# Softmax quotients on GpSimd, two heads in one tile, and another placing of DSA's top-k rounds

## The chip, the cores and the metric

One core of a Trainium2 chip runs the whole kernel. The metric is device time in microseconds, the median of several runs; lower is better. The engines named here are TensorE (PE; its weight loads are shown as PEld), VectorE (DVE), ScalarE (ACT), GpSimd (POOL) and SyncE (SP), which issues the loads.

## The reference, cut to what matters

Two layers; each is a half-step SwiGLU FFN, a mixer of three attention groups, and a second FFN. Sequence length is 256, width 1024, sixteen heads of 64.

```
x = x + 0.5 * swiglu(rmsnorm(x, ffn1_norm), ...)
h = rmsnorm(x, mix_norm);  p = h @ w_in
  A (8 heads): window of 128 keys, learned sink in the softmax sum
  B (4 heads): MoBA; with 256 keys this is plain causal attention
  C (4 heads): DSA; score = sum_h relu(q_idx_h . k_idx) * w_idx_h
               idx = top_k(score, 64 keys); softmax over those keys only
  softmax: e = exp(s - m);  o = (e / sum(e)) @ v
x = x + concat(A, B, C) @ w_out
x = x + 0.5 * swiglu(rmsnorm(x, ffn2_norm), ...)
```

The choice of 64 keys is made in eight rounds on a score tile `acc`: a round finds the eight largest of each row and overwrites them with a marker. After the eighth round the marked places are the chosen keys.

## The kernel before, in words

All arithmetic is in float32. A weight chunk of 128x1024 is split into a high part (`whi`, a cast on ACT) and a low part (`wlo`, a subtraction on DVE that reads `raw` and `whi`), three chunks ahead of its products on PE. The FFNs are long rows of such products (`pgu`, `pdn`).

The mixer (`mix`) is written as one order of work. First come the products for the values (`pv`), five projections (`pp`), and the four index heads (`pi`, `r`, `acc`). Then a loop goes over eight pairs of heads, i = 0 to 7. In one pass of it, `score(i)` issues the score products `psc` on PE, the sum with the bias and the row extreme on DVE (`sb`, `nm`), and the exponentials on ACT (`e`, with the row sums `den`). `values(i-2)` multiplies the transposed weights with the values (`po`) and copies them out (`ohl`). `work(n)` lets PE go on with a number of steps of the remaining projections, later of the output product (`pp`, `pwo`); twelve such steps lie in one pass. `flip(i-1)` transposes the divided exponentials of the previous pair on PE (`pt`, six transposes) and copies them on ACT (`et`). `take(n)` runs rounds of the key choice on DVE. `normalise(i)` adds the sink's term (`es`, `ee`, `dn`), takes the reciprocal `rd`, and divides the exponentials: four DVE instructions per pair, in line 580, two heads by two query blocks. The wider block holds 256 keys and the other 128, so one head's `e` has 384 columns.

Pairs 6 and 7 are group C. Their biases `bs` are the bias plus the mask `sel` made from the finished `acc` (POOL, line 536; `chosen` in line 490). In the pass with the last round, `sel` and the biases of pair 6 are issued. The latent of group C (`latent`) runs beside the loop in three steps: the square `sq` on ACT and `cg` on DVE, then its row sum `pss` and the products `pk` on PE, then `kc` and its values.

Each engine works through its own instructions strictly in program order. That order is made from the code's order when the kernel is built: the scheduler may pull an instruction forward on its engine, but once built it is fixed, and an instruction that waits holds up those behind it. PE's instructions are chained in the order of the code.

Of the kernel before, what the change touches and what calls it, by code (L numbers as in the profile page):

```python
# [10 lines left out]
F32 = mybir.dt.float32  # L11
F32R = mybir.dt.float32r
AF = mybir.ActivationFunctionType
OP = mybir.AluOpType

P = 128
# [12 lines left out]
NKEEP = min(256, T // 4)  # L29
# [15 lines left out]
PRE = 6  # L45
FILL = [12] * 8 + [3, 3, 6]

TAKES = [2, 2, 1, 1, 1, 1, 0, 0]


_QA, _KA, _VA, _QB, _KB, _VB, _QC, _CKV, _QI, _KI, _WI = (
# [26 lines left out]
def tile_trunk(ctx, tc, xT, gains, kvg, sinks, table, onehot, wgu, wdn, winv, wins, wkv, wout, out):  # L78
    nc = tc.nc
# [4 lines left out]
    tmp = ctx.enter_context(tc.tile_pool(name="tmp", bufs=3))  # L84
# [3 lines left out]
    def bank(name, tag="mm"):  # L88
        return psum.tile([P, 512], F32, tag=tag, name=name)
# [100 lines left out]
    ident = const.tile([P, P], F32, name="ident")  # L190
# [15 lines left out]
    def in_order(ins):  # L206
        last_pe[0] = behind(ins, last_pe[0])

    def matmul(*a, **kw):
        in_order(nc.tensor.matmul(*a, **kw))  # L210

    def transpose(*a):
        in_order(nc.tensor.transpose(*a))  # L213
# [155 lines left out]
    bias = const.tile([P, NH, 2 * P], F32, name="bias")  # L369
# [34 lines left out]
    def mix(l, norm, nxt):  # L404

        pv = [bank("pv"), bank("pv")]
        for k in range(DK):
            if k % 2 == 0:
                whi, wlo = next_w()
            c = slice(k % 2 * VCOLS, (k % 2 + 1) * VCOLS)  # L410
# [48 lines left out]
        blocks = ((1, slice(0, T)), (0, slice(T, T + P)))  # L459
# [19 lines left out]
        def take(rounds):  # L479

            for _ in range(rounds):
                for b, cs in blocks:
                    m8 = tmp.tile([P, 8], F32, tag="m8", name="m8", bufs=4)
                    nc.vector.max(out=m8, in_=acc[:, cs])  # L484
                    nc.vector.match_replace(out=acc[:, cs], in_to_replace=m8, in_values=acc[:, cs], imm_value=TAKEN)  # L485

        def chosen():

            sel = tmp.tile([P, 3 * P], F32, tag="sel", name="sel", bufs=1)
            nc.vector.tensor_scalar(sel, acc, TAKEN, NEG, op0=OP.is_gt, op1=OP.mult)  # L490
            return sel
# [25 lines left out]
        nms, dens, ets, sels = {}, {}, {}, {}  # L517
        es_, state = {}, {}

        def qkv(j):  # L520
            h = HEADS[j]
            if h < NA:
                return halves(pr[f"qa{h % 4}"], h // 4), halves(pr["ka"], h // 4), h // 4
            i = h % 4
            if h < NA + NB:
                return halves(pr[f"qb{i // 2}"], i), halves(pr[f"kb{i // 2}"], i), 2 + i
            return halves(pr[f"qc{i // 2}"], i), halves(pr["kc"], i), 6
# [13 lines left out]
        def score(i):  # L541

            nms[i] = tmp.tile([P, 2, 2], F32, tag="nm", name="nm", bufs=3)
            dens[i] = tmp.tile([P, 2, 2], F32, tag="den", name="den", bufs=3)
            ps = [bank("psc", "at") for _ in range(2)]
            both = [qkv(2 * i + m) for m in range(2)]
            for p, (q, k, _) in zip(ps, both):
                matmul(p[:, 0:T], q[:, P:T], k[:, 0:T], start=True, stop=True)
            for p, (q, k, _) in zip(ps, both):
                matmul(p[:, T:T + P], q[:, 0:P], k[:, 0:P], start=True, stop=True)  # L550
            es_[i] = []
            for m, p in enumerate(ps):
                j = 2 * i + m
                sb = tmp.tile([P, 3 * P], F32, tag="A", name="sb")
                for (b, cs), bt in zip(blocks, sels.pop(j)):
                    nc.vector.tensor_tensor_reduce(  # L556
                        out=sb[:, cs], in0=p[:, cs], in1=bt, scale=-1.0,
                        scalar=BIG if j >= NA else nsink[:, l * NA + j:l * NA + j + 1],
                        op0=OP.add, op1=OP.min, accum_out=nms[i][:, b, m:m + 1])
                e = tmp.tile([P, 3 * P], F32, tag="E", name="e", bufs=4)  # L560
                for b, cs in blocks:
                    nc.scalar.activation(e[:, cs], sb[:, cs], AF.Exp, scale=-1.0, bias=nms[i][:, b, m:m + 1],  # L562
                                         accum_out=dens[i][:, b, m:m + 1])
                es_[i].append(e)

        def normalise(i):
            den = dens[i]
            if 2 * i < NA:
                es = tmp.tile([P, 2, 2], F32, tag="es", name="es", bufs=2)
                c = l * NA + 2 * i  # L570
                nc.vector.tensor_add(es, nms[i], sink[:, None, c:c + 2].to_broadcast([P, 2, 2]))
                ee = tmp.tile([P, 2, 2], F32, tag="ee", name="ee", bufs=2)
                nc.scalar.activation(ee, es, AF.Exp)
                den = tmp.tile([P, 2, 2], F32, tag="dn", name="dn", bufs=2)
                nc.vector.tensor_add(den, dens[i], ee)
            rd = tmp.tile([P, 2, 2], F32, tag="rd", name="rd", bufs=2)
            nc.vector.reciprocal(rd, den)
            for m, e in enumerate(es_[i]):
                for b, cs in blocks:
                    nc.vector.tensor_scalar(e[:, cs], e[:, cs], rd[:, b, m:m + 1], None, op0=OP.mult)  # L580

        def flip(i):

            ets[i] = []
            pts = [bank("pt", "at") for _ in range(2)]
            for pt, e in zip(pts, es_.pop(i)):
                for n, c in enumerate((2, 0, 1)):
                    transpose(pt[:, n * P:(n + 1) * P], e[:, c * P:(c + 1) * P], ident)
            for pt in pts:
                et = tmp.tile([P, 3 * P], F32, tag="ET", name="et", bufs=4)  # L590
                nc.scalar.copy(et, pt[:, :3 * P])
                ets[i].append(et)
# [52 lines left out]
        def work(n):  # L645
            for _ in range(n):
                next(fill, None)

        lat = None
        work(PRE)  # L650
        for i in range(NPAIR):
            for j in (2 * i, 2 * i + 1):
                if j not in sels:
                    biases(j)
            score(i)
            if i > 1:
                values(i - 2)
            n = FILL[i]
            work(n // 2)
            if i:  # L660
                flip(i - 1)
            take(TAKES[i])
            if i == len(TAKES) - TAKES[::-1].index(next(t for t in TAKES[::-1] if t)) - 1:
                state["sel"] = chosen()
                biases(NA + NB)
                biases(NA + NB + 1)
            normalise(i)
            if lat is None and "ckv" in pr:
                lat = latent()
            if lat:  # L670
                next(lat, None)
            work(n // 4)
            if lat:
                next(lat, None)
            work(n - n // 2 - n // 4)
# [8 lines left out]
        for k in range(DK):  # L684
            for i in range(LASTK):
                n = k * LASTK + i
# [127 lines left out]
```

## Time and profile before

| quantity | value |
|---|---|
| median of 3 runs | 981.63 us (979.8 to 982.25) |
| the profiled execution | 978.45 us |
| its span | 976.7 us |
| PE busy | 955.7 us, 98% of the span |
| DVE busy | 703.9 us, 72% |
| ACT busy | 536.9 us, 55% |
| POOL busy | 166.0 us, 17% |

The profile is of one execution. Busy time is summed over a whole span, so a share says little on a stage: the mixer of layer 0 lies at 200 to 297 us, that of layer 1 at 676 to 774 us, and the rest is FFN. In the lists below a line gives an instruction's start, its length, engine, line of the kernel, what it writes and reads with the tile's shape, and in brackets how long the engine had been idle before it and what ended that.

### The profile page before, as it was taken

What the parts mean: (1) busy time and instruction counts of PE and PEld (TensorE: products, weight loads), DVE (VectorE), ACT (ScalarE), POOL (GpSimd) and SP (SyncE); (2) the same over time, 40 slices, a digit from 0 to 9 for tenths busy, and PEclk for the clock granted to TensorE, in tenths of its full rate; (3) what the DMA queues carried; (4) which work ended last, traced back from release to release, by engine and by line L of the source; (5) the groups of instructions that cost most, each with busy time, mean ns of one, the idle gap of its engine ahead of it and who ended that gap; (6) DMA issues with size and microseconds to landing.
All of it is one profiled execution on the core that took longest, in us unless ns stands there. A gap on an engine that the chain in (4) does not pass through costs nothing.

```text
span 976.7 us, 15686 instructions
## 1 busy us (share of the span) xinstructions
PE 955.7 (98%) x5920; PEld 845.4 (87%) x5920; DVE 703.9 (72%) x1307; ACT 536.9 (55%) x988; POOL 166.0 (17%) x169
## 2 busy tenths in 40 slices
PE   8999999999999999999999999999999999999996
PEld 6888888898898888888888888889988988888885
DVE  5877776669956877776668777665797578787552
ACT  6655555445656656554456555544465576565442
POOL 3211110100103211211122212111002042122111
PEclk9999999999999999999999999999999999999998
DMA  9697555553434555555545555555433445555511
GB/s 339 232 310 262 205 173 181 183 186 115 142 107 138 209 195 194 176 210 174 199 151 211 176 206 181 177 179 185 150 130 99 161 143 202 197 191 178 208 46 43
DMA packets 47575, 174.41 MB, mean 179 GB/s; under 512 B 3291, under 2 KB 5867, under 8 KB 47372
## 3 DMA queue, kind: packets, MB, share of 16 engines
q1 hardware_dynamic: 47212, 172.90, 51.5%
q8 instruction: 46, 0.75, 0.3%
q10 hardware_dynamic: 288, 0.52, 0.1%
q14 instruction: 29, 0.24, 0.1%
HBM read 172.34 MB, written 4.22 MB: 181 GB/s over the span
## 4 chain that ended last, share of the span: by engine, by line
PE 86%; DVE 6%; ACT 3%; issue 2%; POOL 2%; DMA 1%; SPq 0%; POOLq 0%; DVEq 0%; ACTq 0%
PE pgu L210 46%; PE pdn L210 25%; PE pp L210 6%; PE pwo L210 4%; PE pv L210 2%; DVE wlo L153 2%; ACT whi L152 2%; PE po L210 1%; PE psc L210 1%; PE pt L213 1%; POOL ss L240 1%; POOL rcol L255 1%; DVE acc L485 1%; DMA raw<-wgu 1%; DVE m L484 1%
## 5 line engine op out<-in xcount | busy, mean ns | idle before, releaser
L210 PE MATMUL pgu<-xx,whi 128*128 128x512 f32 x1408 | 494.8, 396 | 2.1 <-DVE xx L230 1.6
L153 DVE TENSOR_TENSOR wlo<-raw,whi 128x1024 fp32r<-128x1024 f32 (+2 forms) x322 | 388.5, 1208 | 147.4 <-ACT whi L152 140.0
L152 ACT CAST whi<-raw 128x1024 fp32r<-128x1024 f32 (+2 forms) x322 | 332.7, 1035 | 254.0 <-PE pdn L210 109.2
L210 PE MATMUL pgu<-xx,wlo 128*128 128x256 f32 x1408 | 395.2, 281 | 0.2 <-DVE wlo L153 0.2
L210 PEld LDWEIGHTS pgu<-xx,whi 128*128 128x128 f32 x1408 | 264.1, 188 | 64.5 <-ACT whi L152 3.4
L210 PEld LDWEIGHTS pgu<-xx,wlo 128*128 128x128 f32 x1408 | 266.3, 189 | 1.1 <-DVE wlo L153 1.0
L210 PE MATMUL pdn<-h,whi 128*128 128x512 f32 x704 | 248.1, 397 | 0.0
L210 PE MATMUL pdn<-h,wlo 128*128 128x256 f32 x704 | 197.5, 281 | 0.0
L210 PEld LDWEIGHTS pdn<-h,whi 128*128 128x128 f32 x704 | 132.1, 188 | 31.2
L336 POOL TENSOR_TENSOR sr<-s,rrow 128x256 f32<-128x256 f32 x88 | 95.6, 1086 | 360.6 <-ACT s L334 360.5
L210 PEld LDWEIGHTS pdn<-h,wlo 128*128 128x128 f32 x704 | 133.2, 189 | 0.0
L288 ACT COPY b<-pgu 128x256 f32<-128x256 f32 x176 | 65.3, 372 | 86.4 <-PE pgu L210 86.4
L290 DVE TENSOR_TENSOR a<-pgu,b 128x256 f32<-128x256 f32 x176 | 73.5, 419 | 26.3 <-ACT b L288 26.0
L210 PE MATMUL pp<-xx,whi 128*128 128x256 f32 x480 | 92.1, 292 | 0.0
L210 PEld LDWEIGHTS pp<-xx,whi 128*128 128x128 f32 x480 | 75.4, 194 | 2.7 <-issue 1.7
L210 PE MATMUL pp<-xx,wlo 128*128 128x256 f32 x240 | 68.5, 285 | 0.0
L240 POOL TENSOR_TENSOR ss<-ss,sq 128x256 f32<-128x256 f32 x41 | 42.1, 1028 | 151.6 <-ACT sq L235 122.2
L338 DVE TENSOR_TENSOR h<-sr,a 128x256 f32<-128x256 f32 x88 | 37.4, 425 | 28.2 <-POOL sr L336 27.7
L210 PE MATMUL pwo<-ohl,whi 128*128 128x256 f32 x256 | 47.7, 287 | 0.0
L210 PEld LDWEIGHTS pp<-xx,wlo 128*128 128x128 f32 x240 | 46.5, 194 | 0.0
L340 ACT CAST h<-h 128x256 fp32r<-128x256 f32 x88 | 35.2, 400 | 14.8 <-DVE h L338 14.8
L562 ACT ACTIVATE e<-sb,nm 128x256 f32<-128x256 f32 x64 | 28.4, 446 | 25.0 <-DVE nm L556 25.0
(97 smaller groups left out, 671.7 us busy)
## 6 DMA issues: line engine op xcount, KB each, us to landing
raw<-wgu SPq DMA_DIRECT2D x86, 1024.0 KB, 4.9
raw<-wdn SPq DMA_DIRECT2D x44, 1024.0 KB, 4.9
raw<-wins SPq DMA_DIRECT2D x14, 1024.0 KB, 4.9
raw<-wout SPq DMA_DIRECT2D x8, 1024.0 KB, 4.9
raw<-winv SPq DMA_DIRECT2D x4, 776.0 KB, 4.3
w<-u SPq DMA_DIRECT2D x1, 3072.0 KB, 14.0
bias<-w SPq DMA_DIRECT2D x1, 2048.0 KB, 9.2
raw<-wgu SPq DMA_DIRECT2D x3, 512.0 KB, 7.6
```

Source lines behind the costliest of these rows:

```text
L152: ops = (nc.scalar.copy(hi[:, a:b], raw(n, a, b)), nc.vector.tensor_sub(lo[:, a:b], raw(n, a, b), f(hi[:, a:b])))
L153: nc.vector.tensor_sub(lo[:, a:b], raw(n, a, b), f(hi[:, a:b])))
L210: in_order(nc.tensor.matmul(*a, **kw))
L213: in_order(nc.tensor.transpose(*a))
L240: nc.gpsimd.tensor_add(s, self.sums[0], sq)
L255: nc.gpsimd.tensor_tensor(out=col, in0=v, in1=mhalf, op=OP.pow)
L288: nc.scalar.copy(b, p[:, T:])
L290: nc.vector.tensor_add(a, p[:, :T], b)
L336: nc.gpsimd.tensor_mul(sr, s, row)
L338: nc.vector.tensor_mul(h, sr, u)
L340: nc.scalar.copy(hs[i][:, 0, :], h)
L562: nc.scalar.activation(e[:, cs], sb[:, cs], AF.Exp, scale=-1.0, bias=nms[i][:, b, m:m + 1], accum_out=dens[i][:, b, m:m + 1])
```

## The change

The exponentials of both heads of a pair go to one tile of 128 x 2 x 384 (two buffers) in place of one tile per head (four buffers). The division leaves DVE: it is now two products on GpSimd, one per query block, each over both heads, with the reciprocal broadcast along the keys. The rounds of the key choice are placed differently in the code: one ahead of the loop, then one in each of the passes 0 to 5, with a second one in pass 5; and `normalise(i)` comes behind the first round of its pass instead of behind all of them.

```diff
-TAKES = [2, 2, 1, 1, 1, 1, 0, 0]
+TAKES = [1, 1, 1, 1, 1, 2, 0, 0]
...
-            es_[i] = []
+            es_[i] = tmp.tile([P, 2, 3 * P], F32, tag="E", name="e", bufs=2)
...
-                e = tmp.tile([P, 3 * P], F32, tag="E", name="e", bufs=4)
                 for b, cs in blocks:
-                    nc.scalar.activation(e[:, cs], sb[:, cs], AF.Exp, scale=-1.0, bias=nms[i][:, b, m:m + 1],
+                    nc.scalar.activation(es_[i][:, m, cs], sb[:, cs], AF.Exp, scale=-1.0, bias=nms[i][:, b, m:m + 1],
                                          accum_out=dens[i][:, b, m:m + 1])
-                es_[i].append(e)
...
-            for m, e in enumerate(es_[i]):
-                for b, cs in blocks:
-                    nc.vector.tensor_scalar(e[:, cs], e[:, cs], rd[:, b, m:m + 1], None, op0=OP.mult)
+            for b, cs in blocks:
+                e = es_[i][:, :, cs]
+                nc.gpsimd.tensor_mul(e, e, rd[:, b, :, None].to_broadcast([P, 2, (1 + b) * P]))
...
-            for pt, e in zip(pts, es_.pop(i)):
+            e = es_.pop(i)
+            for m, pt in enumerate(pts):
                 for n, c in enumerate((2, 0, 1)):
-                    transpose(pt[:, n * P:(n + 1) * P], e[:, c * P:(c + 1) * P], ident)
+                    transpose(pt[:, n * P:(n + 1) * P], e[:, m, c * P:(c + 1) * P], ident)
...
+        take(NKEEP // 8 - sum(TAKES))
         work(PRE)
...
-            take(TAKES[i])
+            take(min(TAKES[i], 1))
+            normalise(i)
+            take(TAKES[i] - 1)
...
-            normalise(i)
```

PE's order stays as it was. On DVE everything up to the reciprocal of pair 0 keeps its order too, five rounds of the key choice among it. From that reciprocal on, the order differs. First DVE at pair 0 (`rd_2511` before, `rd_2510` now), before:

```order
L577 RECIPROCAL rd_2511<-dn_2509 128x4
L556 ISA sb_2550,nm_2542<-psc_2544,bias_124,nsink_93 128x256
L556 ISA nm_2542 128x1
L580 TENSOR_SCALAR e_2458<-e_2458,rd_2511 128x256
L580 TENSOR_SCALAR e_2458<-e_2458,rd_2511 128x128
L580 TENSOR_SCALAR e_2464<-e_2464,rd_2511 128x256
L580 TENSOR_SCALAR e_2464<-e_2464,rd_2511 128x128
L556 ISA sb_2550,nm_2542<-psc_2544,bias_124,nsink_93 128x128
```

And the same place on DVE in the changed kernel:

```order
L575 RECIPROCAL rd_2510<-dn_2508 128x4
L556 ISA sb_2548,nm_2539<-psc_2541,bias_124,nsink_93 128x256
L556 ISA nm_2539 128x1
L556 ISA sb_2548,nm_2539<-psc_2541,bias_124,nsink_93 128x128
L556 ISA nm_2539 128x1
L556 ISA sb_2553,nm_2539<-psc_2542,bias_124,nsink_93 128x256
L556 ISA nm_2539 128x1
L556 ISA sb_2553,nm_2539<-psc_2542,bias_124,nsink_93 128x128
L556 ISA nm_2539 128x1
L448 SCALAR_TENSOR_TENSOR pr6_2526<-pp_2532,rrow_2258 128x256
L569 TENSOR_TENSOR es_2595<-nm_2539,sink_92 128x4
```

The four divisions are gone from DVE, and the score sums of pair 1 (`sb_2548`, `sb_2553`) follow the reciprocal directly; behind `es_2595` stands a `wlo`. On POOL the divisions of pairs 0 to 2 stand between the mask on `acc` and the first biases, where there was only the latent's `rcol`, and the biases of pair 6 stand behind pair 2:

```order
L578 TENSOR_TENSOR e_2461<-e_2461,rd_2510 128x2x256
L578 TENSOR_TENSOR e_2461<-e_2461,rd_2510 128x2x128
L578 TENSOR_TENSOR e_2547<-e_2547,rd_2601 128x2x256
L578 TENSOR_TENSOR e_2547<-e_2547,rd_2601 128x2x128
L578 TENSOR_TENSOR e_2638<-e_2638,rd_2706 128x2x256
L578 TENSOR_TENSOR e_2638<-e_2638,rd_2706 128x2x128
L536 TENSOR_TENSOR bs_3034<-bias_124,sel_3032 128x256
L536 TENSOR_TENSOR bs_3036<-bias_124,sel_3032 128x128
```

The wide block is divided first on POOL, then the narrow one. Next is DVE at the reciprocal of pair 2, up to the first score sum of pair 3 (`sb_2759` before, `sb_2745` now), before:

```order
L577 RECIPROCAL rd_2719<-dn_2717 128x4
L484 MAX m8_2936<-acc_2228 128x8
L580 TENSOR_SCALAR e_2653<-e_2653,rd_2719 128x256
L580 TENSOR_SCALAR e_2653<-e_2653,rd_2719 128x128
L580 TENSOR_SCALAR e_2659<-e_2659,rd_2719 128x256
L580 TENSOR_SCALAR e_2659<-e_2659,rd_2719 128x128
L153 TENSOR_TENSOR wlo83_2739<-raw41_2346,whi83_2738 128x1024
L556 ISA sb_2759,nm_2751<-psc_2753,bias_124,nsink_93 128x256
```

And in the changed kernel:

```order
L575 RECIPROCAL rd_2706<-dn_2704 128x4
L448 SCALAR_TENSOR_TENSOR pr8_2663<-pp_2669,rrow_2258 128x256
L490 TENSOR_SCALAR sel_3032<-acc_2228 128x384
L153 TENSOR_TENSOR wlo83_2724<-raw41_2346,whi83_2723 128x1024
L556 ISA sb_2745,nm_2736<-psc_2738,bias_124,nsink_93 128x256
```

The key choice is finished by then: the mask `sel` stands here, directly behind the reciprocal, and no longer just ahead of pair 4's score sums. Last, ACT at the exponentials of pair 3 and the latent's square `sq`, before:

```order
L603 CAST ohl_2776<-po_2771 128x256
L562 ACTIVATE e_2762,den_2752<-sb_2759,nm_2751 128x256
L562 ACTIVATE e_2762,den_2752<-sb_2759,nm_2751 128x128
L562 ACTIVATE e_2768,den_2752<-sb_2765,nm_2751 128x256
L562 ACTIVATE e_2768,den_2752<-sb_2765,nm_2751 128x128
L573 ACTIVATE ee_2819<-es_2817 128x4
L591 COPY et_2807<-pt_2799 128x384
L591 COPY et_2809<-pt_2800 128x384
L497 ACTIVATE sq_2829<-pr10_2797 128x256
L152 CAST whi84_2833<-raw42_2426 128x1024
```

And in the changed kernel:

```order
L561 ACTIVATE e_2744,den_2737<-sb_2745,nm_2736 128x256
L561 ACTIVATE e_2744,den_2737<-sb_2745,nm_2736 128x128
L561 ACTIVATE e_2744,den_2737<-sb_2750,nm_2736 128x256
L561 ACTIVATE e_2744,den_2737<-sb_2750,nm_2736 128x128
L602 CAST ohl_2760<-po_2755 128x256
L571 ACTIVATE ee_2803<-es_2801 128x4
L152 CAST whi84_2815<-raw42_2432 128x1024
L590 COPY et_2791<-pt_2783 128x384
L590 COPY et_2793<-pt_2784 128x384
L497 ACTIVATE sq_2811<-pr10_2781 128x256
```

The copy `ohl` now stands behind the four exponentials, and the weight cast `whi84` has moved from behind `sq` to ahead of it.

## Rows read from the trace of the kernel before

**Rows 1.** The profile's page, busy time of each engine.
```profile
PE 955.7 (98%) x5920; PEld 845.4 (87%) x5920; DVE 703.9 (72%) x1307; ACT 536.9 (55%) x988; POOL 166.0 (17%) x169
```
**Rows 2.** Waits of PE, whole span: line waited for, us in total, times, longest.
```profile
PE pt L213 <- DVE e L580: 4.0, 2, 2.0
```
**Rows 3.** Busy time by stretch, layer 0: PE, PEld, DVE, ACT, POOL, clock, DMA.
```profile
242.00:250.00 8.00, 8.00 (x74) 7.06 (x70) 8.00 (x34) 4.97 (x14) 0.00 (x0) 1.00 0.38 132
```
**Rows 4.** Timeline of DVE at pair 0: start, length, instruction, idle before.
```profile
237.55 0.17 DVE L577 RECIPROCAL rd<-dn 128x4 f32<-128x4 f32 x1
238.02 1.00 DVE L580 TENSOR_SCALAR e<-e,rd 128x256 f32<-128x256 f32 x4
239.88 0.42 DVE L448 SCALAR_TENSOR_TENSOR pr<-pp,rrow 128x256 f32<-128x256 f32 x1
```
**Rows 5.** Timeline of PE at the transposes of pairs 0 and 1.
```profile
238.62 1.01 PE L213 MATMUL pt<-ident,e 128*128 128x128 f32 x6 [2.01 <-DVE e L580]
239.38 0.49 PE L210 MATMUL pp<-xx,whi 128*128 128x256 f32 x2
...
245.60 0.82 PE L213 MATMUL pt<-ident,e 128*128 128x128 f32 x6
246.18 0.48 PE L210 MATMUL pp<-xx,whi 128*128 128x256 f32 x2
```
**Rows 6.** Groups of POOL's instructions by shape, 250 to 280 us: busy, mean ns.
```profile
L536 POOL TENSOR_TENSOR bs<-bias,sel 128x256 f32<-128x256 f32 x4 | 2.9, 734 | 14.8 <-DVE nm L556 13.0 <-DVE sel L490 1.8
L536 POOL TENSOR_TENSOR bs<-bias,sel 128x128 f32<-128x128 f32 x4 | 1.8, 456 | 0.0
```
**Rows 7.** Timeline of POOL in the mixer of layer 0.
```profile
225.59 0.41 POOL L476 TENSOR_SCALAR_AFFINE_SELECT acc<-acc 128x256 f32<-128x256 f32 x1 [15.51 <-DVE acc L473]
...
257.59 2.27 POOL L536 TENSOR_TENSOR bs<-bias,sel 128x256 f32<-128x256 f32 x4 [1.82 <-DVE sel L490]
```
**Rows 8.** Timeline of POOL and DVE where sums of squares meet weight splits.
```profile
311.70 0.73 POOL L240 TENSOR_TENSOR ss<-ss,sq 128x256 f32<-128x256 f32 x1
...
312.51 1.60 POOL L240 TENSOR_TENSOR ss<-ss,sq 128x256 f32<-128x256 f32 x1
...
313.44 1.76 DVE L153 TENSOR_TENSOR wlo<-raw,whi 128x1024 fp32r<-128x1024 f32 x1
```
**Rows 9.** Timeline of DVE, pairs 2 to 5.
```profile
243.10 0.48 DVE L556 CUSTOM_DVE_ANT_0 sb<-psc,bias,nsink 128x256 f32<-128x256 f32 x1
...
248.30 0.17 DVE L577 RECIPROCAL rd<-dn 128x4 f32<-128x4 f32 x1
...
249.47 1.22 DVE L153 TENSOR_TENSOR wlo<-raw,whi 128x1024 fp32r<-128x1024 f32 x1
250.61 0.48 DVE L556 CUSTOM_DVE_ANT_0 sb<-psc,bias,nsink 128x256 f32<-128x256 f32 x1
...
257.15 0.36 DVE L490 TENSOR_SCALAR sel<-acc 128x384 f32<-128x384 f32 x1
...
265.38 0.42 DVE L556 CUSTOM_DVE_ANT_0 sb<-psc,bias 128x256 f32<-128x256 f32 x1
```
**Rows 10.** Timeline of PE, pairs 2, 3 and 5, and the latent's row sum.
```profile
241.70 0.92 PE L210 MATMUL psc<-pr,pr 64*128 64x256 f32 x8
...
248.50 0.92 PE L210 MATMUL psc<-pr,pr 64*128 64x256 f32 x8
...
254.20 0.61 PE L210 MATMUL pss<-ones,sq 128*128 128x1 f32 x4
...
264.45 0.93 PE L210 MATMUL psc<-pr,pr 64*128 64x256 f32 x8 [0.56 <-DVE pr L448]
```
**Rows 11.** Timeline of ACT around the exponentials of pair 3.
```profile
250.27 0.37 ACT L603 CAST ohl<-po 128x256 fp32r<-128x256 f32 x1 [1.45 <-PE po L210]
...
253.72 0.42 ACT L497 ACTIVATE sq<-pr 128x256 f32<-128x256 f32 x1
254.04 1.04 ACT L152 CAST whi<-raw 128x1024 fp32r<-128x1024 f32 x1
```

## The prediction

> **What bounds the kernel now.** I read the busy times first, then what PE waited for, then the mixer by stretches, and last the instructions around PE's two waits. PE is busy for 955.7 of 976.7 us [rows 1]; DVE and ACT are far from that. So a change pays only where PE waits, and costs only where it makes PE wait. Of PE's waits two kinds lie in the lines that the change touches. One is at the transposes of pair 0, for the divisions on DVE: 4.0 us in two waits, one per layer [rows 2]. The other is at the score products of pair 5, 0.56 us, for a projection's product on DVE [rows 10]; the second layer runs the same order. Between them DVE is full, 8.00 of 8.00 us, but so is PE [rows 3]: DVE's load costs nothing there. All that the change can give back is thus 2.0 and 0.56 us per layer.
>
> **The divisions.** Per layer DVE loses 32 instructions, four per pair at 1.00 us for the four [rows 4]; PE's own work covers them except at pair 0. POOL gains 16. A product with two operands in SBUF takes POOL 734 ns on 256 columns and 456 ns on 128 [rows 6], so 2.17 ns a column more, and 512 columns (two heads, wide block) are estimated at 1.29 us. With 0.73 for the narrow block a pair takes 2.02 us. No broadcast operand was seen: the lower bound is the one-operand rate of 0.41 us per 256 columns [rows 7], 1.23 us a pair; the upper is a product that waits for another engine (below). I take 2.02, the same operation on the nearest shapes. POOL starts 0.08 us after a DVE result: `sel` at 257.15 with 0.36 [rows 9], `bs` at 257.59 [rows 7].
>
> **Pair 0.** The order on DVE up to the reciprocal is unchanged, with the same five rounds ahead of it, so the new placing of rounds brings that reciprocal no earlier: it starts at 237.55 and takes 0.17 [rows 4]. POOL divides from 237.80 to 239.82. The transposes start with the narrow block, POOL's second product, so they start 0.06 later, at 239.88, in place of 238.62. The next projection follows them by 0.58 us where they do not wait (245.60 to 246.18) and by 0.76 where the divisions trickle in [rows 5]: it comes at 240.46 in place of 239.38. That is 1.08 us per layer, in full on PE's path.
>
> **Do DVE and POOL disturb each other?** One `ss` on POOL took 0.73 us and the one behind it, started within a `wlo`, 1.60; the next `wlo`, started within that `ss`, took 1.76 [rows 8] against 1.22 [rows 9]. So 0.54 late, at 313.98, it got through 0.13 before that `ss` ended: each waits for the other's instruction, until 0.13 us before its reported end. At pair 0 DVE reaches `es` and the `wlo` behind it at 239.30 (the `pr` of 239.88 less 0.91 for the divisions, and its own 0.33). POOL's second product starts at 239.09, ahead of them by 0.21, and is taken as undisturbed.
>
> **Pairs 2 and 3.** Here `sel` and a `wlo` now stand behind the reciprocal, beside POOL's division, and the score sum of pair 3 behind them. Set out from PE, moved by 1.08: the score products of pair 2 at 242.78, the sum 0.93 later (264.45 to 265.38 [rows 9, 10], where DVE was free), 243.71. The reciprocal was 5.20 behind that sum (243.10 to 248.30 [rows 9]); its list now has one `pr` less and one short match more, and stays at 5.20: 248.91. From that reciprocal on, in us behind it: POOL's wide product from 0.25 lets others through at 0.25 + 1.29 - 0.13 = 1.41. DVE has `pr` from 0.09 to 0.42, and `sel` wants to start. No row shows a `sel` beside a POOL product; its wait lies between 0 and 0.99, and I take the whole, after `wlo`, which like it reads and writes SBUF. Then `sel` runs to 1.69 (0.28), POOL's waiting narrow product holds `wlo` until 2.29, and `wlo` with 1.14 (249.47 to 250.61) ends at 3.43: the sum of pair 3 starts at 252.34. Before, this stretch took 2.31.
>
> The Trainium skill has a rule on just this (page "SBUF — State Buffer", section "Who interferes with whom"): a DVE instruction with two SBUF inputs contends with a GpSimd instruction that reads SBUF, and `tensor_scalar` in its two-port mode contends too; the later one blocks fully. The `ss` and `wlo` rows agree (1.60 against 0.73); the `sel` part no row here shows. By the rule the sum is the one below, without its second half it is the rival at 985.7.
>
> **The latent's row sum.** ACT's chain from that score sum to `sq` took 3.11 us (250.61 to 253.72) [rows 9, 11]. Now `ohl` (0.37) and `whi` (1.04) [rows 11] stand within it, 1.21 with 0.1 of overlap each. PE's `pss` came 0.48 after the start of `sq` [rows 10, 11], with almost no slack. So `pss` can start at 252.34 + 3.11 + 1.21 + 0.48 = 257.14; PE would be there at 254.20 + 1.08 = 255.28. A new wait of 1.86 us per layer.
>
> **Pair 5.** The 0.91 us that DVE saves ahead of the late `pr` would end the wait of 0.56, but a `wlo` stands between, next to POOL's wide product that can hold it for up to 1.16. The result lies between -0.56 and +0.25; I take 0, since both come from the same reciprocal.
>
> **The rest at nothing.** The other pairs' transposes come 3 us or more behind their reciprocal; 2.02, or 3.2 with one `wlo` between, fits. POOL has 16.2 us more per layer and stands nearly idle in the mixer [rows 3]. The biases of pair 6 are made early, those of pair 7 only 2.27 us [rows 7]. The exponential tiles take the same space; one SP load of the latent's weights changes places with a weight load, hundreds of us ahead of its use. If POOL were late elsewhere, PE would wait for it one to one.
>
> **Sum.** 1.08 + 1.86 + 0 = 2.94 us per layer, 5.9 for both. On the profiled execution that is 978.45 + 5.9 = 984.3; the median of the runs lies 3.2 above that execution, so the forecast is 981.63 + 5.9 = 987.5 us.
>
> **The rivals.**
> - *`sel` does not wait.* `wlo` is then held only until 1.41, the sum of pair 3 starts at 251.46, `pss` waits 0.98: 2.06 per layer, 985.7 us. For it: no row shows `sel` held.
> - *No engine holds the other.* The sum of pair 3 starts at 250.75, `pss` waits 0.27 and pair 5 gives its 0.56 back: 0.79 per layer, 983.2 us. Against it: the 1.60 and 1.76 of [rows 8].
> - *Not slower.* The GpSimd product with a broadcast operand runs at the one-operand rate, 1.23 us a pair, and nothing is held. Pair 0 then costs 0.29, `pss` 0.27, and pair 5 returns 0.56: 981.6 us. It decides in this direction from about 1.2 us a pair; the 734 ns of [rows 6] speak against it.
> - *`wlo` slips between the two products of pair 0.* The margin is 0.21 us: a wide product of 1.5 us would let `es` and `wlo` in at 239.37, the narrow one would run from 240.46 to 241.19, and the next projection would come at 241.83, 2.45 late. With 0.25 more at `sel`: 2.45 + 2.11 = 4.56 per layer, 990.7 us. For it: the wide product's length is only extended from shorter ones.
>
> **How the numbers follow.** Chances: forecast 0.42, `sel` free 0.17, nothing held 0.13, not slower 0.11, `wlo` between 0.17. What a measurement of this kernel can tell from no change is about 0.3%, 2.9 us: slower begins at 984.6, faster ends at 978.7. Slower gets the forecast, the slipped `wlo` and most of the free `sel`, 0.71. Within 0.3% come nothing held, a part of not slower and of the free `sel`, 0.22. Faster can come only from more than the 0.56 per layer that PE still waits at pair 5, which no row offers, and keeps 0.07. The range reaches from 982.3, which takes in the case where nothing is held, to 991, which takes in the slipped `wlo`; the case of no loss and a still slower POOL are left out.
>
> **What would show it.** PE's wait at the transposes of layer 0 grows from 2.0 to about 3.3 us and is for POOL's division; a wide product takes about 1.3 and a narrow one 0.73; `sel` takes over 1 us; PE waits at `pss` for `sq`, 1 to 2 us; pair 5's wait stays near 0.5. The prediction is wrong if the divisions take under 1.3 or over 3 us a pair, or if `pss` does not wait.

## The result: 986.25 us, slower by half a per cent, and the profile after

The changed kernel takes 986.25 us (median of 5 runs, 984.79 to 986.7); the kernel before took 981.63 (5 runs, 978.63 to 982.5). The ratio is 1.0051, with a 95% interval from 1.0034 to 1.0069: 3.3 to 6.8 us slower. The forecast was 987.5. The profiled execution took 984.79 us, its span 983.0.

The page's first part, to lay beside [rows 1]: DVE gave up 10 us of work and POOL took on 36.

```profile
PE 957.9 (97%) x5920; PEld 846.2 (86%) x5920; DVE 693.7 (71%) x1243; ACT 536.7 (55%) x988; POOL 201.6 (21%) x201
```

PE's waits in the lines that the change touches, as in [rows 2]: line waited for, us in total, times, longest.

```profile
PE pt L213 <- POOL e L578: 5.9, 2, 2.9
...
PE pss L210 <- ACT sq L497: 2.9, 2, 1.5
...
PE psc L210 <- DVE pr L448: 0.5, 1, 0.5
PE psc L210 <- ACT whi L152: 0.4, 1, 0.4
```

The wait at the transposes of pair 0 has grown from 2.0 to 2.9 us and is now for POOL. The wait at the latent's row sum is new. The small one at pair 5 stayed in layer 0; in layer 1 PE waits 0.4 us there for ACT's `whi` instead.

POOL's divisions by shape, first in the pair that nothing disturbs (pair 0), and below it in the whole mixer of layer 0 (from 225 to 290 us). Columns as in [rows 6].

```profile
L578 POOL TENSOR_TENSOR e<-e,rd 128x512 f32<-128x512 f32 x1 | 1.0, 1038 | 11.9 <-DVE rd L575 11.9
L578 POOL TENSOR_TENSOR e<-e,rd 128x256 f32<-128x256 f32 x1 | 0.6, 611 | 0.0
...
L578 POOL TENSOR_TENSOR e<-e,rd 128x512 f32<-128x512 f32 x8 | 9.1, 1139 | 36.7 <-DVE rd L575 30.1 <-PE pwo L210 4.6 <-ACT et L590 1.9
L578 POOL TENSOR_TENSOR e<-e,rd 128x256 f32<-128x256 f32 x8 | 8.0, 994 | 0.0
```

A pair takes 1.04 + 0.61 us undisturbed, less than the 1.29 + 0.73 of the forecast, and more where DVE works beside it: the narrow product's mean is 994 ns over the mixer.

PE at pair 0, as in [rows 5]:

```profile
236.24 0.88 PE L213 MATMUL pt<-ident,e 128*128 128x128 f32 x6 [2.93 <-POOL e L578]
236.87 0.48 PE L210 MATMUL pp<-xx,whi 128*128 128x256 f32 x2
...
240.69 0.70 PE L210 MATMUL psc<-pr,pr 64*128 64x256 f32 x4
```

From the next projection to the score products of pair 2 it is now 240.69 - 236.87 = 3.82 us; before it was 241.70 - 239.38 = 2.32 [rows 5, 10]. The same products take 1.50 us more. The windows tell why; the number behind the last busy column is the granted clock as a share of 2.4 GHz. The changed kernel behind this wait, layer 0:

```profile
237.50:239.00 1.50, 1.50 (x9) 1.50 (x8) 1.50 (x10) 0.29 (x2) 0.00 (x0) 0.50 0.37 33
239.00:240.70 1.70, 1.70 (x11) 1.48 (x9) 0.44 (x2) 0.00 (x0) 1.61 (x2) 0.51 0.91 352
240.70:246.00 5.30, 5.30 (x48) 4.82 (x48) 4.36 (x20) 3.77 (x13) 0.00 (x0) 1.00 0.20 80
```

And the kernel before behind its wait of 2.0 us, layer 0 and then layer 1:

```profile
240.00:241.70 1.70, 1.70 (x16) 1.57 (x15) 1.70 (x6) 1.42 (x7) 0.00 (x0) 1.00 0.37 152
...
715.50:717.00 1.50, 1.50 (x9) 1.50 (x9) 1.50 (x5) 1.50 (x8) 0.00 (x0) 0.50 0.60 246
```

Behind the wait PE runs at its lower level, 1.2 GHz, until 240.7 us: 9 products in 1.5 us where the kernel before got 16 into 1.7. Before, the drop came in layer 1 only. A wait can thus cost once while PE stands and again behind it; the prediction counted the first alone.

DVE behind the reciprocal of pair 2, as in [rows 9], where `sel` and a `wlo` now stand:

```profile
246.81 0.17 DVE L575 RECIPROCAL rd<-dn 128x4 f32<-128x4 f32 x1
...
247.22 1.19 DVE L490 TENSOR_SCALAR sel<-acc 128x384 f32<-128x384 f32 x1
248.33 1.63 DVE L153 TENSOR_TENSOR wlo<-raw,whi 128x1024 fp32r<-128x1024 f32 x1
249.88 0.47 DVE L556 CUSTOM_DVE_ANT_0 sb<-psc,bias,nsink 128x256 f32<-128x256 f32 x1
```

And POOL beside it, as in [rows 7]:

```profile
247.15 1.73 POOL L578 TENSOR_TENSOR e<-e,rd 128x512 f32<-128x512 f32 x2 [6.46 <-DVE rd L575]
```

The two products of that row apart (columns as in [rows 6]):

```profile
L578 POOL TENSOR_TENSOR e<-e,rd 128x512 f32<-128x512 f32 x1 | 1.0, 1041 | 6.5 <-DVE rd L575 6.5
L578 POOL TENSOR_TENSOR e<-e,rd 128x256 f32<-128x256 f32 x1 | 0.7, 728 | 0.0
```

`sel` took 1.19 us, where it took 0.36 alone [rows 9]: POOL's wide product ends at 248.19, and `sel` 0.22 us behind it. `wlo` took 1.63 in place of 1.22, beside the narrow one. The Trainium skill's rule (page "SBUF — State Buffer", section "Who interferes with whom"), by which a `tensor_scalar` in its two-port mode contends with GpSimd too, was cited in the prediction with the remark that no row here shows that part; these rows agree with it. So the score sum of pair 3 came 3.07 us behind the reciprocal (3.43 forecast, 2.31 before).

The chain then went through ACT, as in [rows 11], to PE, as in [rows 10]:

```profile
254.26 0.42 ACT L497 ACTIVATE sq<-pr 128x256 f32<-128x256 f32 x1
```

```profile
254.73 0.61 PE L210 MATMUL pss<-ones,sq 128*128 128x1 f32 x4 [1.47 <-ACT sq L497]
```

From that score sum to `sq` it took 4.38 us (3.11 + 1.21 = 4.32 forecast), and PE stood 1.47 us.

### The profile page after: what moved, and what is told of

Read it like the earlier page. It is cut to its first block, busy times and chain, and to the rows that moved or that the text cites. A ratio compares the mean times of both kernels' runs of the same rounds, so it can differ in the third digit from the quotient of the medians.

```text
span 983.0 us, 15686 instructions
## 1 busy us (share of the span) xinstructions
PE 957.9 (97%) x5920; PEld 846.2 (86%) x5920; DVE 693.7 (71%) x1243; ACT 536.7 (55%) x988; POOL 201.6 (21%) x201
## 4 chain that ended last, share of the span: by engine, by line
PE 84%; DVE 6%; ACT 3%; issue 2%; POOL 2%; DMA 1%; SPq 0%; POOLq 0%; DVEq 0%; ACTq 0%
PE pgu L210 46%; PE pdn L210 24%; PE pp L210 5%; PE pwo L210 4%; DVE wlo L153 2%; PE pv L210 2%; ACT whi L152 2%; DMA raw<-wgu 1%; PE psc L210 1%; PE po L210 1%; DVE acc L485 1%; PE pt L213 1%; DVE sb L556 1%; POOL rcol L255 1%; DVE m L484 1%
## 5 line engine op out<-in xcount | busy, mean ns | idle before, releaser
L578 POOL TENSOR_TENSOR e<-e,rd 128x512 f32<-128x512 f32 (+1 forms) x32 | 33.5, 1067 | 74.8 <-DVE rd L575 61.6
```

Source lines behind the costliest of these rows:

```text
L578: nc.gpsimd.tensor_mul(e, e, rd[:, b, :, None].to_broadcast([P, 2, (1 + b) * P]))
```

## The experiments

A mixer's length, from the start of the score products of pair 0 to the start of the transposes of pair 7, tells more of a single profile than its span: the FFNs vary by themselves (last section). The table adds both layers. Waits are PE's, per layer; ratios are to the kernel before run on the same chip, with their 95% interval (medians there 981.49 us for the first four rows of experiments and 980.36 for the next four, 982.31 for the last four). An edit in the code also lets the scheduler order the engines anew: only where `pss` alone moved did DVE, ACT and POOL keep their order, and with `sel` on POOL only `sel` changed its place. The other edits reordered DVE, some of them ACT; where it matters the text says so.

| kernel | median us | ratio [95%] | wait at `pt`, pair 0 | at `pss` | two mixers |
|---|---|---|---|---|---|
| before | 981.63 | | 2.0 | none | 119.15 |
| changed | 986.25 | 1.0051 [1.0034, 1.0069] | 2.9 | 1.5 | 126.26 |
| all division on DVE | 981.42 | 1.0000 [0.9979, 1.0020] | 2.0 | none | 120.57 |
| `sel` on POOL | 986.66 | 1.0061 [1.0038, 1.0085] | 2.9 | 0.6 | 124.26 |
| PE filled at pair 0 | 987.12 | 1.0071 [1.0051, 1.0090] | 0.7 | 2.0 | 125.73 |
| `pss` later | 983.69 | 1.0034 [1.0018, 1.0051] | 2.9 | 0.4 | 121.29 |
| pair 0 divided on DVE | 983.68 | 1.0041 [1.0016, 1.0065] | 2.0 | 0.8 | 122.22 |
| rounds tied | 978.78 | 0.9998 [0.9970, 1.0025] | 0.8 | 1.2 | 118.38 |
| rounds tied, DVE divides | 984.08 | 1.0041 [1.0021, 1.0062] | none | 0.9 | 121.72 |
| DVE divides, rounds earlier | 989.61 | 1.0098 [1.0062, 1.0134] | none | 1.7 | 126.14 |
| rounds tied, `pss` later | 976.98 | 0.9949 [0.9931, 0.9967] | 0.8 | none | 114.61 |
| rounds tied, `pss` later, `pt` 2 steps later | 971.34 | 0.9897 [0.9869, 0.9925] | none | none | 112.32 |
| before, `pt` 5 steps later | 977.59 | 0.9951 [0.9933, 0.9968] | 0.2 | 0.7 | 115.91 |
| changed, `pt` 6 later, `pss` later | 977.66 | 0.9947 [0.9927, 0.9968] | 0.8 | 0.7 | 116.05 |

**All division back on DVE.** The shared tile and the new placing of the rounds stay.

```diff
-            for b, cs in blocks:
-                e = es_[i][:, :, cs]
-                nc.gpsimd.tensor_mul(e, e, rd[:, b, :, None].to_broadcast([P, 2, (1 + b) * P]))
+            for m in range(2):
+                for b, cs in blocks:
+                    e = es_[i][:, m, cs]
+                    nc.vector.tensor_scalar(e, e, rd[:, b, m:m + 1], None, op0=OP.mult)
```

> One tile for two heads and the new placing of rounds are kept; the division goes back to four products on VectorE. Theory (the loss comes from the division on GpSimd: a later transpose of pair 0, a held sel, and PE's clock falling after longer waits): PE's wait at the transposes is back at 2.0 us per layer from 2.9, sel takes 0.36 us again from 1.19, PE waits under 0.3 us at the latent's row sum, and the time is that of before, 981 to 982 us. Rival (the new placing of the rounds and the shared tile cost by themselves): it stays 2 us or more above before, with a wait at the row sum.

The time is that of the kernel before (981.42 against 981.49), and so is the wait:

```profile
PE pt L213 <- DVE e L579: 4.0, 2, 2.0
```

So the shared tile and the code's new placing cost nothing that shows (the interval reaches 2 us either way), and the loss comes with the division on GpSimd. It comes with the order that the scheduler makes of it, too: with DVE dividing, `sel` is back just ahead of pair 4's score sums and takes 0.36 us. The clock fell behind the 2.0 us wait in both layers here, which is the 1.4 us by which the two mixers are longer than before.

**Only pair 0 back on DVE.**

```diff
+            if i == 0:
+                for m in range(2):
+                    for b, cs in blocks:
+                        e = es_[i][:, m, cs]
+                        nc.vector.tensor_scalar(e, e, rd[:, b, m:m + 1], None, op0=OP.mult)
+            else:
...
```

Behind `else` stand the two products on GpSimd, as they were.

> Only the division of pair 0 goes back to DVE (four products on the shared tile); pairs 1 to 7 stay with GpSimd. The scheduler then also puts `sel` behind the score sum of pair 3, where it can no longer hold `sq`. Theory (the loss is two places, pair 0 and `sel` beside the division of pair 2, and the other six pairs cost nothing): PE's wait at the transposes is 2.0 us per layer as in the kernel before, the wait at `pss` is under 0.6, and the time is 981.5 to 983 us. Rival (the 1.6 to 2.6 us of GpSimd in every pair cost PE something throughout): the time stays at 984 us or more with the first two waits gone.

Between theory and rival (983.68 us):

```profile
PE pt L213 <- DVE e L580: 4.0, 2, 2.0
PE pss L210 <- ACT sq L497: 1.7, 2, 0.8
```

Pair 0 is as before, but `pss` still waits 0.84 us in layer 0 although `sel` stands behind the score sum there: `wlo` beside the division of pair 2 took 1.47 us, and on ACT `ohl` and `whi` still stand ahead of `sq`. So of the 1.47 us of wait about 0.6 go with the changed place of `sel`, not all. No other pair shows a new wait.

**`sel` made on GpSimd.**

```diff
-            nc.vector.tensor_scalar(sel, acc, TAKEN, NEG, op0=OP.is_gt, op1=OP.mult)
+            nc.gpsimd.tensor_scalar(sel, acc, TAKEN, NEG, op0=OP.is_gt, op1=OP.mult)
```

> The mask sel is made on GpSimd instead of VectorE; everything else is in the order of the changed kernel. Theory (sel and the weight split behind it are held by the division on GpSimd, and through the score sums of pair 3 and ScalarE's chain they make PE wait at the latent's row sum): the split starts about 0.8 us earlier, PE's wait at the row sum falls from 1.47 to about 0.7 us per layer, and the time falls by 1.5 us against the changed kernel, to 984 to 985 us, more where PE's clock no longer falls behind that wait. Rival (ScalarE's new order alone makes that wait): the wait stays at 1.3 us or more, and the time at 986 us.

```profile
PE pss L210 <- ACT sq L497: 1.2, 2, 0.6
```

The wait fell by 0.9 us per layer and the two mixers by 2.0, but the median did not fall. `wlo` ran undisturbed (1.23 us), but started only 0.5 us earlier behind the reciprocal, not 0.8. So ACT's new order alone does not make the wait: with no instruction of DVE held there, 0.6 us of it are left. The clock's drop at pair 0 was longer in layer 1 (transposes to the score products of pair 2: 5.31 us, against 4.26 in the changed kernel), and the runs spread over 5.4 us. The mechanism is confirmed by the wait; the price is not shown by the time.

**PE filled ahead of pair 0's transposes** with ten products of the identity that nobody reads.

```diff
+FILLER = 10
...
+            if i == 0:
+                for _ in range(FILLER):
+                    matmul(pts[0][:, :P], ident, ident, start=True, stop=True)
```

> Ten products of the identity with itself (output overwritten by the transposes) are put on PE ahead of the transposes of pair 0, in the time in which it waits. Theory (PE's granted clock falls to half after the wait of 2.9 us, and the 18 projection products behind the transposes take 3.6 in place of 2.1 us for that): the transposes start as late as in the changed kernel, but the clock stays at 1.0 behind them, the 18 products take 2.1 to 2.2 us, and the time falls by about 2.7 us, to 983 to 984 us. Rival (the products are slow because the division and the weight split share the memory with them, or because a weight chunk is late): they stay at 3.6 us and the time at 986 us or above.

A miss, and a useful one (the kernel's lines are one further on). The drop behind the transposes is gone (2.95 us to the next score products in both layers), so it was the clock that made the products slow there; but nothing was won:

```profile
PE pss L211 <- ACT sq L498: 4.0, 2, 2.0
```

Counted from the score products of pair 0, PE reached `pss` 1.5 us earlier than in the changed kernel and `sq` came only 1.0 earlier (the scheduler had also put `sel` ahead of pair 2's reciprocal here, where it took 0.36). So PE stood there longer, and now the clock fell behind that wait in both layers; in layer 0:

```profile
255.00:258.10 3.10, 3.10 (x15) 2.87 (x13) 0.00 (x0) 0.00 (x0) 1.47 (x3) 0.50 0.87 252
```

From `pss` to the score products of pair 4 it took 4.05 us there in place of 2.59. Busy work moved both prices to the next late result.

**The latent's row sum three projection steps later on PE.**

```diff
             work(n // 4)
+            work(n - n // 2 - n // 4)
             if lat:
                 next(lat, None)
-            work(n - n // 2 - n // 4)
```

> The latent's row sum and products come three projection steps later on PE (1.07 us); the orders of the other engines are those of the changed kernel. Theory (PE's wait at the row sum costs its length, one to one): the wait falls from 1.47 to about 0.4 us per layer, nothing else grows, and the time falls by 2 us against the changed kernel, to 984 us, by up to 1.3 us more if PE's clock no longer falls behind that wait. Rival (what hangs on the score sums of pair 3 only waits elsewhere): PE waits at the score products of pair 4 or 5 instead, and the time stays at 986 us.

As the theory had it: wait 0.40 us, no drop of the clock behind it, 983.69 us. The other engines' orders are unchanged, so this is the cleanest of the tests. The mixers are 5.0 us shorter, but 1.5 of these are no gain of the edit: in layer 0 the clock did not fall behind pair 0's wait, which was as long as before (2.94 us). By the ratios (1.0051 and 1.0034) a third of the loss sits at this one place, by the medians half; the two intervals overlap.

**The rounds tied behind their reciprocal.** In both kernels five of the eight rounds run ahead of the reciprocal of pair 0, but for the last overwriting of the fifth: two are written there in the code, the others the scheduler pulls forward. Here an order of issue holds the rounds of a pass behind the reciprocal of that pass.

```diff
-TAKES = [1, 1, 1, 1, 1, 2, 0, 0]
+TAKES = [2, 2, 1, 1, 1, 1, 0, 0]
...
-                    nc.vector.max(out=m8, in_=acc[:, cs])
+                    behind(nc.vector.max(out=m8, in_=acc[:, cs]), first)
...
-            take(min(TAKES[i], 1))
-            normalise(i)
-            take(TAKES[i] - 1)
+            take(TAKES[i], normalise(i))
```

> Division on GpSimd, but the rounds of the key choice are tied on DVE behind the reciprocal of their own pass (two in pass 0, two in pass 1, one each in passes 2 to 5), so that no round stands ahead of the reciprocal of pair 0, as five do in both kernels. Theory (those five rounds are why PE waits at pair 0 at all): the reciprocal comes 2 to 4 us earlier, PE's wait at the transposes of pair 0 falls from 2.9 to under 0.9 us, the granted clock does not fall behind it, psc of pair 0 to psc of pair 5 takes 36 to 37.5 us per layer, and the time is 977 to 981 us, below the changed kernel by 5 or more. Rival (DVE's work is only moved: rounds run later hold later score sums, and `sel`, now directly ahead of the score sums of pair 6, makes these wait for GpSimd's biases): waits of the same size appear at pairs 2 to 6 and the time stays at 983 to 987.

DVE at pair 0:

```profile
232.73 0.42 DVE L448 SCALAR_TENSOR_TENSOR pr<-pp,rrow 128x256 f32<-128x256 f32 x1 [1.94 <-PE pp L210]
233.07 1.22 DVE L153 TENSOR_TENSOR wlo<-raw,whi 128x1024 fp32r<-128x1024 f32 x1
...
235.41 0.17 DVE L575 RECIPROCAL rd<-dn 128x4 f32<-128x4 f32 x1
```

And PE at the two places:

```profile
237.40 0.88 PE L213 MATMUL pt<-ident,e 128*128 128x128 f32 x6 [0.80 <-POOL e L578]
...
254.40 0.61 PE L210 MATMUL pss<-ones,sq 128*128 128x1 f32 x4 [1.20 <-ACT sq L497]
```

The reciprocal comes 7.43 us behind the score products of pair 0 (at 227.98), in place of 237.55 - 227.99 = 9.56 before [rows 4]; a `pr` that waits for PE and two `wlo` are now what it stands behind. The wait of 2.9 us is down to 0.8, with no drop of the clock behind it. By the ratios (0.9998 and 1.0051) the time lies half a per cent under the changed kernel, and level with the kernel before.

**The same with DVE dividing.** Edit: besides, the four DVE products in place of GpSimd's two.

> The same tie of the rounds, with the division on DVE. Theory (rounds ahead of the reciprocal cause the wait at pair 0, whoever divides): no wait at pair 0's transposes, the time 976 to 979.5 us, below the kernel before by 2 to 5. Rival (the biases of pair 6 come too late behind `sel`): a wait at pair 6 takes the gain back, 981 to 984.

The theory on the time fell (984.08 us). The wait at pair 0 is gone, but others came, and not at pair 6, where the rival had put them:

```profile
244.28 0.55 PE L213 MATMUL pt<-ident,e 128*128 128x128 f32 x3 [0.57 <-ACT et L592]
...
252.41 0.55 PE L213 MATMUL pt<-ident,e 128*128 128x128 f32 x3 [1.11 <-ACT et L592]
...
266.31 0.92 PE L210 MATMUL psc<-pr,pr 64*128 64x256 f32 x8 [1.49 <-DVE pr L448]
```

The window says of what (columns: PE, PEld, DVE):

```profile
246.00:253.00 7.00, 5.89 (x51) 5.04 (x50) 7.00 (x29) 4.57 (x12) 0.00 (x0) 1.00 0.27 83
```

DVE is full and PE no longer is. With the rounds behind the reciprocals DVE has no room for the divisions, and here GpSimd's division is worth about 5 us (978.78 against 984.08, on the same chip; ratios 0.9998 and 1.0041, whose intervals just touch). Against the kernel before neither part gains: the division on GpSimd alone lost 0.5%, the tie alone 0.4%, and the two together came out level.

**The same, DVE dividing, with rounds in passes 0 to 4**, `TAKES = [2, 2, 2, 1, 1, 0, 0, 0]`.

> As the kernel before this one in the list, but with two rounds in each of the passes 0 to 2 and one in passes 3 and 4, so that `sel` and the biases of pair 6 come a whole pass earlier. Theory (a late `sel` costs something at pair 6): no wait for biases, and 0.5 to 2 us below the version with rounds up to pass 5, 975.5 to 979 us. Rival (DVE has no room in pass 2 for a second round): score sums of pairs 2 and 3 come later and PE waits there, same time or slower than with one round in pass 2.

The rival held: the second round of pass 2 made the score sums of pair 3 and `sq` late, `pss` waits 1.70 us, pair 5 1.76, and the time is 989.61 us. A late `sel` had not been the trouble.

**Rounds tied, GpSimd dividing, `pss` three steps later** (both edits above).

> The kernel with GpSimd's division and the rounds tied behind their reciprocals, which ran 0 to 2 us below the kernel before, with the latent's row sum `pss` three projection steps later on PE; nothing else moves on any engine. Theory (its `pss` wait of 1.2 us per layer is lost PE time, and the lower clock behind it in layer 1 goes with it): the wait falls under 0.2 us, 2.4 to 3.5 us less than without this move, 975.5 to 977.5 us. Rival (the wait or the clock's fall goes elsewhere, as with the filled wait at pair 0): no gain, 978 to 980.

No wait is left at `pss`, no drop behind it, and the two layers are alike to 0.01 us (57.31 and 57.30). 976.98 us is below both kernels, as the theory said.

**In addition the transposes of pair 0 two steps later.**

```diff
-            work(n // 2)
+            h = n // 2 + (2 if i == 1 else 0)
+            work(h)
...
+            q = min(n // 4, n - h)
+            work(q)
+            work(n - h - q)
```

> The kernel listed first, with the transposes of pair 0 also two projection steps (about 0.8 us) later on PE, where it had still waited 0.8 us for GpSimd's second product. Theory: no wait of PE left in the mixer from pair 0 to 5 above 0.3 us, and 1 to 1.6 us below the first, 974.5 to 976.5 us. Rival (the copies of the transposes on ACT come later and hold the value products): a wait at `po` or a later `sq` takes it back, same as the first.

All that PE waits for over the whole span:

```profile
PE prow L213 <- POOL rcol L255: 4.3, 4, 1.4
PE pgu L210 <- ACT whi L152: 1.6, 2, 1.1
PE warm L210 <- POOL ident L192: 1.4, 1, 1.4
PE pss L210 <- ACT sq L235: 0.9, 1, 0.9
PE pgu L210 <- DVE wlo L153: 0.2, 1, 0.2
PE pss L210 <- POOL ss L240: 0.2, 1, 0.2
```

Of this at most 0.2 us lies in the loop over the pairs. The windows of the two mixers:

```profile
227.84:284.80 56.96, 56.74 (x480) 51.88 (x480) 44.77 (x165) 36.62 (x105) 22.01 (x25) 1.00 0.38 125
700.87:757.80 56.93, 56.71 (x479) 51.87 (x479) 44.76 (x165) 36.59 (x105) 22.00 (x25) 1.00 0.37 125
```

PE is busy for all but 0.2 us, at 2.4 GHz. This is the fastest version: 971.34 us (6 runs, 968.44 to 974.31), 0.9897 [0.9869, 0.9925] of the kernel before. The waits came out as expected, the time did not: it lies 3 us under the range. Of the 7 to 13 us against the kernel before, 6.8 stand in the two mixers; the rest is not explained by its profile, which is of one of the two slowest of the six runs (see the paces below).

**The kernel before, with the transposes of pair 0 five steps later.** Edit as above, with 5; `pss` keeps its place.

> The kernel before with one edit: the transposes of pair 0 stand five projection steps (about 2 us) later on PE. Theory (the 2.0 us that PE waited there per layer is the only thing in the mixer that the change could have given back): the wait falls under 0.3 us, the clock no longer drops behind it, and the time is 975.5 to 978 us, 4 to 5 below the kernel before. Rival (the five rounds ahead of the reciprocal make everything behind it late, so that the next wait comes at pair 1 or at the latent): a wait of 1 to 2 us shows up there and the time is 979 to 982.

```profile
238.40 1.01 PE L213 MATMUL pt<-ident,e 128*128 128x128 f32 x6 [0.21 <-DVE e L580]
```

This one move gives 4.7 us (0.9951), 3.2 of them in the two mixers: the wait and the drop are gone; 0.7 us per layer came back at `pss`, where the rival had looked for more.

**The changed kernel with PE's order moved**: transposes of pair 0 six steps later, `pss` three.

> The changed kernel with the division on GpSimd and its own placing of rounds, and only PE's order moved: the transposes of pair 0 six projection steps (about 2.35 us) later, directly ahead of the score products of pair 2, and the latent's row sum three steps later. Theory (all that the change lost is PE standing at these two places, and the clock behind them): the wait at the transposes falls to 0.6 us, that at `pss` to 0.4, and the time comes to 976.5 to 979 us, 7 to 10 below the changed kernel and below the kernel before. Rival (the lateness of DVE and GpSimd is passed on to pairs 1 and 2): new waits at the value products of pair 0 or the score sum of pair 2, 981 to 984.

```profile
239.24 0.88 PE L213 MATMUL pt<-ident,e 128*128 128x128 f32 x6 [0.77 <-POOL e L578]
```

977.66 us, level with the experiment before this one, with waits somewhat above the expected ones (0.77 and 0.66 us) and no drop of the clock in either mixer. GpSimd still does every division. But not only PE's order has moved: the scheduler put `sel` behind the score sums of pair 3, where no division holds it:

```profile
251.23 0.36 DVE L490 TENSOR_SCALAR sel<-acc 128x384 f32<-128x384 f32 x1
```

So the loss goes when PE asks later and `sel` is out of the way; that it was PE's standing at these two places alone, and the clock behind them, is likely but not shown by this run. Nor is the comparison like for like: the kernel before with its `pss` moved as well was not run, and by its two waits of 0.7 us it could still gain up to about 1.5 us (an estimate).

## Why the prediction was right, and where it was not

Slower was right, and +5.9 us was forecast where +4.6 was measured. By its own terms, per layer, from the two profiles:

| term | forecast | layer 0 | layer 1 |
|---|---|---|---|
| pair 0, up to the next score products | 1.08 | 0.79, and 1.50 by the clock | 0.59 in all (the clock had fallen there before too) |
| `pss` | 1.86 | 1.54 | 1.58, and 0.69 by the clock |
| pair 5 | 0 | -0.12 | 0.60 (clock still low) |
| mixer | 2.94 | 3.68 | 3.43 |

- *Pair 0.* The mechanism held: same reciprocal, 9.56 us behind the score products in both kernels, a longer division, transposes for POOL. The size was off: two products take 1.65 us, not 2.02. The line drawn through 734 and 456 ns was too steep for this product with a broadcast operand. So the wait rose by 0.92 instead of 1.26.
- *Who holds whom.* The reciprocal of pair 2 came 5.17 us behind its score sum, as forecast (5.20). `sel` was held by POOL's wide product and `wlo` by the narrow one, as chosen; the rivals in which `sel` goes free, or nothing is held, fell with the 1.19 and 1.63 us. The shorter products brought the sum of pair 3 0.36 us nearer to the reciprocal, which is most of the step from 1.86 to 1.54.
- *`wlo` between the products of pair 0* did not happen: the narrow one took its 0.61.
- *Pair 5 and the rest.* Pair 5 gave back 0.12 in layer 0, and what is left of the mixer sums to -0.03 in either layer: no other pair costs anything to speak of.
- *The missing term.* The granted clock, which the prediction put at nothing. It adds 1.5 us behind pair 0 where it falls, and 1.4 behind `pss` in layer 1 (0.69 there, the rest at pair 5). In the profiles it outweighs what the terms were too large by: the two mixers differ by 7.1 us, not 5.9. In the medians most of it seems to fall away, since the kernel before loses the clock behind its own 2.0 us wait in some layers too (one of two in its profile; with all division on DVE it fell in both, and the two mixers took 120.57). Without the clock the terms of layer 0 sum to 2.21, 4.4 for both layers, near the 4.6 measured. That the forecast of 987.5 came so close is thus in part luck: its terms were 0.7 us per layer too large, and the clock was left out.

The largest thing that the prediction did not see is on the other side. It took the five rounds ahead of the reciprocal as given and said that all the change could give back was 2.0 and 0.56 us per layer. The rounds could be held back; PE's order could ask later. Both together, with the division on GpSimd, ran at 0.9897 of the kernel before, some 10 us less, 6.8 of them in the mixers. How much of that needs GpSimd is open: PE's moves were not tried together on a kernel in which DVE divides.

## What to carry to other kernels

A placing in the code is not a placing on the engine: where a scheduler may pull work forward, look at the order it made, and tie what has to stay behind. When the fullest engine waits for one late result, compare making it earlier with asking for it later; moving six transposes by a few steps gave more here (0.9951) than the division on GpSimd and the tied rounds together (0.9998). After every edit look at the order again: one that moves only PE in the code moved DVE's `sel` too. Price a wait of the matmul engine with the clock behind it.

## What the runs showed of the hardware

*The clock behind a wait.* In the pair loops of these 14 profiles, PE's waits of up to 1.1 us were not followed by a lower clock; of those of 1.2 us and over some were. Behind the 2.0 us wait at pair 0 it fell in five of six layers (one of two before, four of four in the experiments with DVE at pair 0), behind 2.9 us also in five of six (changed kernel, `sel` on POOL, `pss` later; in layer 1 of the changed kernel it fell half a us before the wait ended). Behind 1.5 to 2.0 us at `pss` it fell in four of six layers (changed kernel, PE filled, rounds earlier), behind 1.5 to 1.8 us at pair 5 in none of four (the two kernels with rounds tied and DVE dividing). Behind 1.2 us at `pss`, with the rounds tied, in layer 1 only:

```profile
730.00:733.00 3.00, 3.00 (x20) 2.72 (x21) 1.04 (x7) 0.00 (x0) 2.25 (x3) 0.79 0.86 321
```

What decides it in a given layer is open.

*Two paces of the same FFN.* The products of an FFN's second half ran at one of two speeds, both with a granted clock of 1.00. From the profile of the kernel before, layer 0, its two FFNs:

```profile
L210 PE MATMUL pdn<-h,whi 128*128 128x512 f32 x176 | 62.2, 399 | 0.0
...
L210 PE MATMUL pdn<-h,whi 128*128 128x512 f32 x176 | 61.1, 391 | 0.0
```

The second FFN of layer 0 took 124.66 us from its first `pgu` to its first `pdn` and 61.18 for its `pdn` in the kernel before, and 126.77 and 62.35 us in the kernel with all division on DVE: 3.3 us more for the same work. Which pace comes changes from profile to profile and from FFN to FFN, with no wait of PE in it. The twelve runs of the kernel before with `pt` 5 steps later lie at 974.7 to 975.6, at 977.0 to 978.2 and at 981.0 us, steps of about 3 us; so the pace is likely most of the spread of the runs, and a reason why mixers and medians agree here only to a few us. Its cause is open.

*GpSimd's product with a broadcast operand* took 1.04 us for 512 columns and 0.61 for 256, less than the 0.73 of a product of two full tiles of 256 columns [rows 6]. Whether the broadcast is the reason no run shows.
